# Narrow value products first behind transposes, sample sums in three pieces, and position products placed inside output products, in a two-layer encoder

## The chip, the cores and the metric

The kernel runs on 1 core of a Trainium2 chip. The metric is the device time of one execution in microseconds. The engines are named as in the profile: PE is TensorE (matmuls and transposes), PEld its weight loads, DVE is VectorE, ACT is ScalarE, POOL is GpSimd, SP is SyncE, which issues most DMAs.

## What is computed

Two sequences, 2048 prompt rows and 512 sample rows of 1024 float32 channels, go through two layers and a final norm:

```
h = rmsnorm(x, g);  z = h @ w_in            # layer 0: q, k, v, gate
o = banded_gqa_with_sink(q, k, v, ...)      # 16 heads, 4 kv heads, |i-j| <= 128
x = x + (o * silu(gate)) @ w_out
h = rmsnorm(x, g)                           # layer 1: 4 groups of 256 channels
f = fftn(h by group, axes=(positions, channels), norm="ortho").real
x = x + (f * silu(h @ w_gate)) @ w_out
y = rmsnorm(x, final_norm)
```

## The kernel before

Every float32 operand of a large product is split into a high part (a cast to the matmul's format on ACT) and a low part (the difference, on DVE), and each product is made of three matmuls: high by high, high by low, low by high (`matmul3`, L131 to L136; its rows are at L134).

**Attention.** Five chunks of 512 positions; the first is the sample. A chunk has 19 steps, and inside a step a table fixes the order of the pieces on every engine: first half of the values (AV1), transposes of the probabilities S of the next pair of blocks (T0, L709), second half of the values (AV2), scores (L650), the softmax pieces, and projection products that fill in between. The transposed probabilities are split into `pts`. The value products (`values`, L728 to L773, matmul at L767) work on the two halves of the 128 rows at the same time. Their weights are the values v, and for each block of keys two forms occur: part 0 loads 128 weight columns (high and low part of v) and multiplies with the high part of `pts`; part 1 loads 64 weight columns (the high part of v) and multiplies with the low part. They add up in `av`, the wide ones in 128 rows, the narrow ones in the first 64. The order of a half is the list at L745: the middle block wide, the far, the edge, then the three narrow ones. In the second half (`swap`) each half of the rows works for the other of the two blocks.

**Fourier.** Positions are transformed by radix-4 sums of 16 (prompt) or 4 (sample) residue classes, each an array of 128 x 1024. Pairs of classes are handled in turn: `gates(pr, hooks)` makes the products of one pair with the work of others hung in at numbered hooks, `z_odd_even` and L1402 make the channel transform, `combine` (L1599) joins two pairs by `radix4` (group 0: the sample) or `radix4_relative` and stores the sums by POOL DMAs in DRAM. Later, for each class k1, `position` (L1694) makes the position transform: `halves_of` splits the input into `gp` (cast at L1685 on ACT, difference at L1686 on DVE), products `ABp` (L134) go to PSUM, ACT copies (L1719), DVE combines (L1723 to L1726) and multiplies by the stored gate (L1729): the result is `up`. `step` (L1957) makes the positions of its arguments, then `finish` (L1762) for the class before, whose output products are `fo` (48 matmuls at L134 for 128 rows, with weights `tTu`; the weight pieces `wo0` to `wo15` are the moving operand), with the residual added at L1776 and the final norm at L1746. Then `up` is transposed on PE (L112) and split again (L1270 ACT, L1271 DVE). `emit` calls `step` for 0 and 8, then 4, then 2. The sums e, f, r0 and the differences G[4] for these classes are DVE operations at L1519.

In this phase the instructions are put in order by a scheduler, except where `seq` or `after(instruction, other)` fixes it; each engine runs its own in that order.

Of the kernel before, what the change touches and what calls it, by code (L numbers as in the profile page):

```python
# [55 lines left out]
def encoder(  # L56
# [147 lines left out]
    def attention_phase():  # L204

        with ExitStack() as es:
# [403 lines left out]
            def attention(c, p, res, uTs):  # L610
# [117 lines left out]
                def values(b):  # L728
# [12 lines left out]
                    def reached(i, h):  # L741
# [3 lines left out]
                        order = [(1, 0), (far, 0), (edge, 0), (1, 1), (edge, 1), (far, 1)]  # L745
                        rows = ahead = slice(64 * h, 64 * h + 64)
# [12 lines left out]
                    def half(swap):  # L759
                        todo = [reached(h ^ swap, h) for h in range(2)]  # L760
# [472 lines left out]
    def fourier_phase(tail):  # L1233
        with ExitStack() as es:
# [14 lines left out]
            def zt(name):  # L1249
                return right([P, D], F32, name)  # L1250
# [267 lines left out]
            def tt(out, a, b, op):  # L1518
                DVE.tensor_tensor(out, a, b, op)  # L1519
# [11 lines left out]

            def radix4(z, name):

                e = zt(f"e{name}")
                tt(e, z[0], z[2], ALU.add)
                tt(z[0], z[0], z[2], ALU.subtract)
                tt(z[2], z[1], z[3], ALU.add)
                tt(z[1], z[1], z[3], ALU.subtract)
                tt(z[3], e, z[2], ALU.subtract)
                tt(e, e, z[2], ALU.add)  # L1540
                return e, z[3], z[0], z[1]

# [56 lines left out]
            def combine(pr):  # L1599

                if pr.n % 2 == 0:
                    return
                gi = pr.n // 2
                r = (radix4_relative if pr.n > 1 else radix4)(pairs[pr.n - 1].zs + pr.zs, f"r{gi}")
# [3 lines left out]
                for i in range(4):  # L1608
                    POOL.dma_start(gsd[i] if gi == 0 else evd[gi - 1, i] if i < 2 else odd[gi - 1, i - 2], r[i])

            kept = []

# [22 lines left out]
            for n, pr in enumerate(pairs[:-1]):  # L1635
                nx = pairs[n + 1]

                def ahead_of(n, i):
# [5 lines left out]

                gates(pr, {
                    1: [lambda: turns1(nx)], 2: [lambda: turns2(nx)], 3: [lambda: turns3(nx)], 4: [lambda: turns4(nx)],
# [47 lines left out]
            def position(name, tab, gr, gs, tiles, loads=None, parts=None, between=None, later=None):  # L1694
# [4 lines left out]
                for hf in range(2):  # L1699
# [4 lines left out]
                    def acc(out, tabs, c0, n):  # L1704
                        for i, (w, t) in enumerate(zip(tabs, ts)):
# [4 lines left out]
                            end = matmul3(out, w, v, i == 0, i == len(ts) - 1)  # L1710
# [51 lines left out]
            def finish(uT, r, between=None):  # L1762
                r0 = r[0]
                x2 = residual(r)
                for half in range(2):
# [4 lines left out]
                    for k in range(KD):  # L1770
# [3 lines left out]
                        )  # L1774
                    xs = x2[:, half * 512 : half * 512 + 512]
# [287 lines left out]
            def emit(*ks):  # L2063
                step(*((f"p{k1}", k1, *G[k1], pair(k1, 16, 0)) for k1 in ks))
# [228 lines left out]
```

## Time and profile before

| what | value |
|---|---|
| runs | 1543.08, 1545.18, 1551.4 us |
| median | 1545.18 us |
| the profiled execution | 1545.72 us, its span 1543.2 us |
| mean granted clock of PE | 0.998 |
| instructions on PE, DVE, ACT, POOL | 13150, 2431, 1921, 616 |

A row of a timeline gives a start, a duration and a group of like instructions by engine, line, operation, `out<-in` and count; in brackets stands how long the engine was idle before it and what released it. The duration of a matmul reaches from its issue to the end of its write, so neighbouring ones overlap, and the pace is read from start to start. A row of groups gives total busy time, mean ns of one, and idle time before it. A row of windows gives the length and the busy time of PE, PEld, DVE, ACT and POOL, then the granted clock (1.00 is full speed), the DMA share and GB/s.

### The profile page before, as it was taken

What the parts mean: (1) busy time and instruction counts of PE and PEld (TensorE: products, weight loads), DVE (VectorE), ACT (ScalarE), POOL (GpSimd) and SP (SyncE); (2) the same over time, 40 slices, a digit from 0 to 9 for tenths busy, and PEclk for the clock granted to TensorE, in tenths of its full rate; (3) what the DMA queues carried; (4) which work ended last, traced back from release to release, by engine and by line L of the source; (5) the groups of instructions that cost most, each with busy time, mean ns of one, the idle gap of its engine ahead of it and who ended that gap; (6) DMA issues with size and microseconds to landing.
All of it is one profiled execution on the core that took longest, in us unless ns stands there. A gap on an engine that the chain in (4) does not pass through costs nothing.

```text
span 1543.2 us, 33658 instructions
## 1 busy us (share of the span) xinstructions
PE 1525.3 (99%) x13150; PEld 1331.4 (86%) x13150; DVE 1124.2 (73%) x2431; ACT 888.4 (58%) x1921; POOL 451.5 (29%) x616
## 2 busy tenths in 40 slices
PE   9999999999999999999999999999999999999998
PEld 7999888999898888988888899888888888788886
DVE  5898665777538776468764477667888878889896
ACT  6788534787237884268862477646656654343353
POOL 2566652422413323215124142222112111011100
PEclk9999999999999999999999999999999999999999
DMA  8677687685856766866649666684667679457852
GB/s 325 229 288 249 230 338 271 219 302 171 317 205 228 243 220 235 300 202 225 228 160 381 226 210 231 215 299 160 240 207 244 212 250 411 154 189 272 297 184 93
DMA packets 100729, 372.70 MB, mean 242 GB/s; under 512 B 11235, under 2 KB 22251, under 8 KB 83420
## 3 DMA queue, kind: packets, MB, share of 16 engines
q1 hardware_dynamic: 82716, 297.38, 55.8%
q0 software_dynamic: 16688, 70.04, 11.6%
q10 hardware_dynamic: 1168, 3.15, 0.6%
q8 instruction: 103, 1.69, 0.4%
q14 instruction: 54, 0.44, 0.1%
HBM read 280.06 MB, written 90.47 MB: 240 GB/s over the span
## 4 chain that ended last, share of the span: by engine, by line
PE 86%; DVE 6%; DMA 4%; ACT 2%; issue 1%; POOL 0%; SPq 0%; POOLq 0%; DVEq 0%; ACTq 0%
PE pj L524 27%; PE W L134 6%; PE pj L134 6%; PE av L767 6%; PE tp L134 5%; PE av L134 5%; PE spt L650 5%; PE spt L134 4%; PE tp L709 3%; PE Wo L134 3%; PE Z L134 3%; PE fo L134 3%; PE z L1402 2%; PE Zo L134 2%; PE X L134 1%; PE ABp L134 1%
## 5 line engine op out<-in xcount | busy, mean ns | idle before, releaser
L524 PE MATMUL pj<-h,wg 64*128 64x512 f32 x1920 | 438.6, 389 | 0.0
L524 PE MATMUL pj<-h,wq 64*128 64x512 f32 x1560 | 378.9, 389 | 1.2 <-DVE qab L568 1.2
L524 PEld LDWEIGHTS pj<-h,wg 64*128 64x128 f32 x1920 | 330.6, 184 | 20.4
L524 PEld LDWEIGHTS pj<-h,wq 64*128 64x128 f32 x1560 | 284.4, 184 | 22.8 <-DVE qab L568 2.7
L677 ACT ACTIVATE S<-S 128x385 f32<-128x385 f32 (+1 forms) x320 | 189.1, 592 | 61.8 <-DVE S L669 42.0
L669 DVE CUSTOM_DVE_ANT_0 S<-spt,b 128x385 f32<-128x385 f32 (+1 forms) x320 | 165.0, 525 | 79.5 <-PE spt L650 78.3
L722 ACT CAST pts<-tp 128x768 fp32r<-128x768 f32 (+1 forms) x160 | 121.2, 758 | 79.5 <-PE av L767 46.2
L726 DVE TENSOR_TENSOR pts<-tp,pts 128x768 fp32r<-128x768 f32 (+1 forms) x160 | 144.1, 900 | 10.7 <-ACT pts L722 10.1
L767 PE MATMUL av<-pts,v 64*128 64x256 f32 (+3 forms) x1680 | 123.8, 267 | 2.4 <-DVE pts L726 2.3
L812 POOL TENSOR_TENSOR uT<-o,uT 128x256 fp32r<-128x256 f32 x75 | 56.9, 758 | 231.3 <-ACT uT L808 230.9
L650 PE MATMUL spt<-kwin,qab 64*128 64x384 f32 (+1 forms) x960 | 119.5, 339 | 0.9 <-DVE S L669 0.7
L134 PE MATMUL fo<-wo,tTu 128*128 128x512 f32 x480 | 115.4, 394 | 0.0
L767 PEld LDWEIGHTS av<-pts,v 64*64 64x64 f32 (+1 forms) x1680 | 108.4, 159 | 7.4 <-DVE pts L726 3.1
L134 PEld LDWEIGHTS fo<-wo,tTu 128*128 128x128 f32 x480 | 89.1, 189 | 18.0
L709 PEld LDWEIGHTS tp<-ident,S 64*128 64x128 f32 x1792 | 86.6, 138 | 10.7 <-DVE pts L726 3.1
L709 PE MATMUL tp<-ident,S 64*128 64x64 f32 x1792 | 91.1, 223 | 0.2 <-DVE pts L726 0.2
L692 DVE TENSOR_SCALAR S<-S 128x384 f32<-128x384 f32 (+1 forms) x192 | 89.1, 493 | 0.1
L803 POOL TENSOR_TENSOR o<-o,s 128x256 f32<-128x256 f32 x75 | 55.6, 741 | 114.7 <-DVE o L797 89.8
L650 PEld LDWEIGHTS spt<-kwin,qab 64*128 64x128 f32 x960 | 81.5, 186 | 3.8 <-issue 1.8
L279 DVE SCALAR_TENSOR_TENSOR h<-xk,g0s,h 128x512 fp32r<-128x512 f32 x40 | 44.9, 1135 | 49.6 <-ACT h L278 49.6
L524 PE MATMUL pj<-wo,uT 64*128 64x512 f32 x360 | 74.6, 390 | 0.0
L278 ACT ACTIVATE h<-xk,g0s 128x512 fp32r<-128x512 f32 x40 | 28.7, 724 | 75.0 <-POOL xk L274 73.8
(376 smaller groups left out, 3358.5 us busy)
## 6 DMA issues: line engine op xcount, KB each, us to landing
wo<-wsd SPq DMA_DIRECT2D x32, 1024.0 KB, 6.5
wq<-wsd SPq DMA_DIRECT2D x31, 1024.0 KB, 6.6
wg<-wsd SPq DMA_DIRECT2D x31, 1024.0 KB, 5.7
x<-x1d SPq DMA_DIRECT2D x40, 512.0 KB, 4.0
b<-b21d SPq DMA_DIRECT2D x40, 512.0 KB, 5.2
b<-rowd SPq DMA_DIRECT2D x40, 384.0 KB, 4.2
xs<-in_x_dram SPq DMA_DIRECT2D x23, 512.0 KB, 6.3
s2d<-gt POOLq DMA_DIRECT2D x40, 256.0 KB, 4.4
```

Source lines behind the costliest of these rows:

```text
L134: ins = pe(PE.matmul(out, a[i], b[j], start=start and i + j == 0, stop=stop and i == 1, skip_group_check=more))
L524: out.last[h] = pe(PE.matmul(out.ps, a[i], b[j], **out.flags()))
L650: pe(PE.matmul(spt[j][:, 2 + k0 * P : 2 + k1 * P], res["q"][rows, qp, b * P : (b + 1) * P], kwin[g][rows, kp, b * P + k0 * P : b * P + k1 ...
L669: seq(DVE, DVE.tensor_tensor_reduce(out=s[:, e0:e1], in0=ps[:, 1 + e0 : 1 + e1], in1=st["bias"][:, j, 386 - e1 : 386 - e0][:, ::-1], scale ...
L677: last_exp[0] = seq(ACT, ACT.activation(s[:, e0:e1], s[:, e0:e1], AF.Exp, bias=s[:, 386:387], scale=-1.0, accum_out=s[:, 387:388]))
L692: seq(DVE, DVE.tensor_scalar(s[:, ks], s[:, ks], den, None, ALU.mult))
L709: pe(PE.transpose(ps[h][:, kb, j, :], s[rows, j, 1 + kb * P : 1 + (kb + 1) * P], ident[rows, rows]))
L722: seq(ACT, ACT.copy(hi, ps))
L726: seq(DVE, DVE.tensor_tensor(lo, ps, f32(hi), ALU.subtract))
L767: last[i][h] = pe(PE.matmul(to, v, pt, start=not swap and n == 0, stop=swap and n == len(todo[h]) - 1, skip_group_check=True,))
L803: eng.tensor_tensor(o, o, s, ALU.mult)
L812: low = eng.tensor_tensor(lo, o, f32(hi), ALU.subtract)
```

## The change

It has three parts.

First, in the second half of the values (`swap`), the list begins with the middle block's narrow product. The list of the first half stays.

```
-                    def reached(i, h):
+                    def reached(i, h, swap):
...
                         order = [(1, 0), (far, 0), (edge, 0), (1, 1), (edge, 1), (far, 1)]
+                        if swap:
+                            order = [(1, 1), (1, 0), (far, 0), (edge, 0), (edge, 1), (far, 1)]
...
-                        todo = [reached(h ^ swap, h) for h in range(2)]
+                        todo = [reached(h ^ swap, h, swap) for h in range(2)]
```

PE's rows at one second half, before (chunk 2, head pair 3; 128x256 and 64x256 are partitions and columns of the output, hence weight columns and streamed columns; v2_5 and v1_4 are the middle blocks):

```order
L709 MATMUL tp_79<-ident_81,S2_3_2_7500 128x64 x12
L767 MATMUL av_80<-pts2_3_0_7441,v2_5_6365 128x256
L767 MATMUL av_80<-pts2_3_0_7441,v1_4_3466 128x256
L767 MATMUL av_80<-pts2_3_0_7441,v2_6_6368 128x256
L767 MATMUL av_80<-pts2_3_0_7441,v1_3_3439 128x256
L767 MATMUL av_80<-pts2_3_0_7441,v1_4_3466 128x2x64
L767 MATMUL av_80<-pts2_3_0_7441,v2_5_6365 128x2x64
L767 MATMUL av_80<-pts2_3_0_7441,v2_5_6365 64x256
L767 MATMUL av_80<-pts2_3_0_7441,v1_4_3466 64x256
```

And after (the line has become L769):

```order
L709 MATMUL tp_79<-ident_81,S2_3_2_7500 128x64 x12
L769 MATMUL av_80<-pts2_3_0_7441,v2_5_6365 64x256
L769 MATMUL av_80<-pts2_3_0_7441,v1_4_3466 64x256
L769 MATMUL av_80<-pts2_3_0_7441,v2_5_6365 128x256
L769 MATMUL av_80<-pts2_3_0_7441,v1_4_3466 128x256
L769 MATMUL av_80<-pts2_3_0_7441,v2_6_6368 128x256
L769 MATMUL av_80<-pts2_3_0_7441,v1_3_3439 128x256
L769 MATMUL av_80<-pts2_3_0_7441,v1_4_3466 128x2x64
L769 MATMUL av_80<-pts2_3_0_7441,v2_5_6365 128x2x64
```

The two narrow products of the middle block have moved from behind the six wide ones to directly behind the transposes. In the attention phase nothing else moves on PE, and nothing on DVE, ACT, POOL or SP.

Second, the sample's sums (six DVE operations and four POOL DMAs) leave `combine` at hook 6 of pair 0's gates and stand in three pieces at hooks 2, 3 and 4 of pair 1's.

```
-                if pr.n % 2 == 0:
+                if pr.n % 2 == 0 or pr.n == 1:
                     return
...
+            def sample_sums(part):
...
+                if part == 0:
+                    tt(e, z[0], z[2], ALU.add)
+                    tt(z[0], z[0], z[2], ALU.subtract)
+                elif part == 1:
+                    tt(z[2], z[1], z[3], ALU.add)
+                    tt(z[1], z[1], z[3], ALU.subtract)
+                else:
+                    tt(z[3], e, z[2], ALU.subtract)
+                    tt(e, e, z[2], ALU.add)
+                    for i, r in enumerate((e, z[3], z[0], z[1])):
+                        POOL.dma_start(gsd[i], r)
...
-                    1: [lambda: turns1(nx)], 2: [lambda: turns2(nx)], 3: [lambda: turns3(nx)], 4: [lambda: turns4(nx)],
+                    1: [lambda: turns1(nx)], 2: [lambda: turns2(nx), lambda: sample_part(0)],
+                    3: [lambda: turns3(nx), lambda: sample_part(1)], 4: [lambda: turns4(nx), lambda: sample_part(2)],
```

In the order that results, DVE's rows there are the same but for one cast (S1_2, L1355), which stands four places earlier, and POOL's stores of the sums stand where they stood.

Third, `step` gets a number n. It issues the loads of its positions and the first casts, and `finish` calls the positions after its n-th output product, with their products tied behind that one (`behind`). The two differences of G[4] follow `emit(10, 0, 8)`, tied behind a DVE combination of the position 8; position 6's first casts move ahead of two sums.

```
-            def finish(uT, r, between=None):
+            def finish(uT, r, between=None, within=None, n=0):
...
+                        if within and half * KD + k + 1 == n:
+                            chain["rows"] = end
+                            within()
+                            chain.pop("rows")
...
-                            end = matmul3(out, w, v, i == 0, i == len(ts) - 1)
+                            end = matmul3(out, w, v, i == 0, i == len(ts) - 1, behind=chain.get("rows"))
...
-            def step(*positions):
-                new = [t for p in positions for t in position(*p)]
-                if pend:
-                    end = finish(*pend.pop(0))
+            def step(n, *positions):
+                new, held = [], []
+                for i, p in enumerate(positions):
+                    held.append((position_loads(p[0], p[1], p[4]), None if i else [halves_of(p[0], p[2], p[3], 0), None]))
+
+                def within():
+                    for p, h in zip(positions, held):
+                        new.extend(position(*p, *h))
+
+                if not n:
+                    within()
+                end = finish(*pend.pop(0), None, within, n)
...
-            e, g4r = pm(w0[0], w0[2], "e0")
-            f, g4s = pm(w0[1], w0[3], "f0")
+            e, f = zt("e0"), zt("f0")
+            for n, a, b in ((e, 0, 2), (f, 1, 3)):
+                tt(n, w0[a], w0[b], A)
             r0, r8 = pm(e, f, "r0")
-            G[0], G[8], G[4] = (r0, None), (r8, None), (g4r, g4s)
-            emit(0, 8)
+            G[0], G[8], G[4] = (r0, None), (r8, None), (w0[0], w0[1])
+            emit(10, 0, 8)
+            for a in range(2):
+                after(tt(w0[a], w0[a], w0[a + 2], S), last_b[0])
...
-            emit(4)
+            emit(0, 4)
...
-            emit(2)
+            emit(3, 2)
...
+            p6 = [halves_of("p6", *G[6], 0), None]
             g1s = zt("g1s")
             tt(g1s, o0s, e0s, A)
             g7s = [half_of(o0s, e0s, lower_half, "g7s0")]
             tt(o0s[:, upper_half], o0s[:, upper_half], e0s[:, upper_half], S)
-            p6 = [halves_of("p6", *G[6], 0), None]
```

PE's rows from the start of the output products of rows 2048 on (`fo2048`), in which positions 0 and 8 fall, before:

```order
L134 MATMUL fo2048_0_17997<-wo0_17430,tTu2048_0_17751 128x512 x3
L134 MATMUL fo2048_0_17997<-wo1_17432,tTu2048_0_17751 128x512
L134 MATMUL ABp0_0_17939<-gp0_0_0_17936,tbp0_17933 128x260
L134 MATMUL fo2048_0_17997<-wo1_17432,tTu2048_0_17751 128x512 x2
L134 MATMUL ABp0_1_17952<-gp0_1_0_17949,tbp0_17933 128x260
L134 MATMUL fo2048_0_17997<-wo2_17454,tTu2048_0_17751 128x512 x3
```

And after, from the tenth weight piece on:

```order
L134 MATMUL fo2048_1_17968<-wo9_17691,tTu2048_0_17751 128x512 x3
L134 MATMUL ABp0_0_17976<-gp0_0_0_17933,tbp0_17931 128x260 x3
L134 MATMUL ABp0_0_17976<-gp0_0_0_17933,tbp0_17931 128x256 x3
L134 MATMUL ABp0_1_17989<-gp0_1_0_17986,tbp0_17931 128x260 x3
L134 MATMUL ABp0_1_17989<-gp0_1_0_17986,tbp0_17931 128x256 x3
L134 MATMUL fo2048_1_17968<-wo10_17722,tTu2048_0_17751 128x512 x3
L134 MATMUL fo2048_1_17968<-wo11_17725,tTu2048_0_17751 128x512
L134 MATMUL ABp8_0_18004<-gp8_0_0_18001,tbp8_17938 128x260 x3
```

The first product of position 0 stood behind 4 of the 48 output products and now stands behind 30; the 12 of position 0 stand together, then 4 output products, the 12 of position 8, and the last 14. In the step of position 4 its 24 products stood together ahead of the next 48 output products; now 5 stand first, and 12 and 10 output products stand between the parts that follow (11 and 8). For position 2, 5 stood ahead of 5 output products and 19 behind; now 9 output products go first and the 24 stand together.

DVE's rows ahead of position 0, before (ev0_0 and ev1_0 are w0[0] and w0[1], e0, f0 and r0 the sums):

```order
L1519 TENSOR_TENSOR e0_17922<-ev0_0_17910,ev2_0_17914 128x1024
L1776 TENSOR_TENSOR x2_2049_17763<-x2_2049_17763,fo2049_1_17791 128x512
L1519 TENSOR_TENSOR ev0_0_17910<-ev0_0_17910,ev2_0_17914 128x1024
L1271 TENSOR_TENSOR tTu2050_0_17842<-tw0_17825,tTu2050_0_17842 128x512
L127 TENSOR_SCALAR invf2049_17820<-ssf2049_17817 128x1
L1519 TENSOR_TENSOR f0_17925<-ev1_0_17912,z11_17370 128x1024
L1746 SCALAR_TENSOR_TENSOR x2_2049_17763<-x2_2049_17763,invf2049_17820,gfb_17400 128x1024
L1271 TENSOR_TENSOR tTu2050_1_17845<-tw0_17825,tTu2050_1_17845 128x512
L1776 TENSOR_TENSOR x2_2051_17848<-x2_2051_17848,fo2051_0_17850 128x512
L1519 TENSOR_TENSOR ev1_0_17912<-ev1_0_17912,z11_17370 128x1024
L1519 TENSOR_TENSOR r0_17928<-e0_17922,f0_17925 128x1024
```

And after, further down, around position 8's gating (up8 times s2p8):

```order
L1740 TENSOR_TENSOR up8_0_18000<-up8_0_18000,ABp8_0_18004 128x2x127
L1740 TENSOR_TENSOR up8_0_18000<-up8_0_18000,ABp8_1_18017 128x2x127
L1741 TENSOR_TENSOR up8_0_18000<-up8_0_18000,ABp8_0_18004 128x2x127
L1741 TENSOR_TENSOR up8_0_18000<-up8_0_18000,ABp8_1_18017 128x2x127
L1521 TENSOR_TENSOR ev0_0_17910<-ev0_0_17910,ev2_0_17914 128x1024
L1744 TENSOR_TENSOR up8_0_18000<-up8_0_18000,s2p8_8_17936 128x1024
```

The two differences in place (ev0_0, ev1_0) stood ahead of r0 and are gone there; the first now stands between position 8's combinations and its gating, the second four rows behind the first. On the other engines the loads of a step's gates and tables are issued earlier: on SP one store of output rows (x2_0) now stands ahead of the load s2p2_2.

More of the change, by code (lines that the diff above doesn't have):

```diff
@@ L1518, in tt @@
             def tt(out, a, b, op):
-                DVE.tensor_tensor(out, a, b, op)
+                return DVE.tensor_tensor(out, a, b, op)
             def radix4_relative(z, name):
@@ L1608, in combine @@
                 for i in range(4):
-                    POOL.dma_start(gsd[i] if gi == 0 else evd[gi - 1, i] if i < 2 else odd[gi - 1, i - 2], r[i])
+                    POOL.dma_start(evd[gi - 1, i] if i < 2 else odd[gi - 1, i - 2], r[i])
             kept = []
+            def sample_sums(part):
+                z = pairs[0].zs + pairs[1].zs
+                if not part:
+                    kept_e.append(zt("er0"))
+                e = kept_e[0]
+                if part == 0:
[9 more added lines that the diff above has]
+                        POOL.dma_start(gsd[i], r)
+            kept_e = []
             pr = pairs[0]
```

18 lines of the change are left out of this document (6 added, 12 removed).

## The prediction

> **What bounds the kernel now.** I read the page's busy times and its chain first, then PE's waits, then the lines by form, and last the timelines at the places that the diff touches.
>
> ```profile
> span 1543.2 us, 33658 instructions
> PE 1525.3 (99%) x13150; PEld 1331.4 (86%) x13150; DVE 1124.2 (73%) x2431; ACT 888.4 (58%) x1921; POOL 451.5 (29%) x616
> PE 86%; DVE 6%; DMA 4%; ACT 2%; issue 1%; POOL 0%; SPq 0%; POOLq 0%; DVEq 0%; ACTq 0%
> PE ABp L134 <- ACT gp L1685: 2.1, 1, 2.1
> PE ABp L134 <- DVE gp L1686: 1.2, 2, 0.8
> PE z L1402 <- DVE s L1348: 1.1, 1, 1.1
> ```
>
> PE is busy for 1525.3 of 1543.2 us and makes up 86% of the chain, so about 18 us (1543.2 − 1525.3) of idle time can go at the most. What a change removes in PE's own stream counts in full; work moved on VectorE (DVE) counts only where PE waits for it. The last three rows (total us, times, longest) are the waits near the edited code: position products for casts, and the columns of pair 2 for a sum. A busy PE can still hold time that weight loads cost, so the next rows are the value products, by tile and shape. The POOL row counts their sites: one such sum for each.
>
> ```profile
> L767 PEld LDWEIGHTS av<-pts,v 64*128 64x128 f32 x840 | 71.7, 186 | 4.3 <-ACT S L690 0.4 <-issue 0.2
> L767 PEld LDWEIGHTS av<-pts,v 64*64 64x64 f32 x840 | 54.8, 132 | 3.1 <-DVE pts L726 3.1
> L803 POOL TENSOR_TENSOR o<-o,s 128x256 f32<-128x256 f32 x75 | 55.6, 741 | 114.7 <-DVE o L797 89.8 <-PE pj L524 24.9
> ```
>
> **Part 1, value products.** One site in the timeline of PE (start, duration of the group, instructions): first half, 12 transposes, second half, scores.
>
> ```profile
> 493.93 0.75 PE L767 MATMUL av<-pts,v 64*128 64x256 f32 x12
> 494.52 0.53 PE L709 MATMUL tp<-ident,S 64*128 64x64 f32 x12
> 494.87 0.84 PE L767 MATMUL av<-pts,v 64*128 64x256 f32 x12
> 495.55 0.69 PE L650 MATMUL spt<-kwin,qab 64*128 64x384 f32 x6
> ```
>
> Both halves stream the same columns. From start to start the first half takes 494.52 − 493.93 = 0.59 us, the second 495.55 − 494.87 = 0.68. The first comes behind 512-column products, long enough to hide its first weight loads; the second comes behind transposes of 64 columns, which hide little. So about 0.09 us of loading lies bare at a site. A 64-column load takes 186 − 132 = 0.054 us less, and the change puts that load first: 75 x 0.054 = 4.05 us. Bounds: nothing (the next, longer load is bare instead) and the whole 0.09, 75 x 0.09 = 6.8 us.
>
> Against it: the second half now goes from 128-wide transposes to a 64-wide product, back to 128 and to 64 again, two more changes of width at a site. The first half contains one such change. The 12 products stream 4 x 256 + 2 x 128 columns at each width, 2560 in all, two at a time on the two halves of the rows: 1280. At the output products' pace of 0.23 us for 512 columns (rows below) that is 0.575 us, so the change of width fits into 0.59 − 0.575 = 0.015 us, about the rounding of the rows. Two at each site would be at most 2.3 us; I take off 0.25 us, near the small end, and keep 2.3 for the range. Part 1: −3.8 us.
>
> The Trainium skill ("TensorEngine Tiling (Array Packing)", section "Key Properties") says that going over to another tiling mode drains TensorE. It speaks against this edit; the first half's 0.59 us shows no drain of a size that matters, but its price is a rival below.
>
> **Part 2, sample sums.** They leave the end of pair 0's gates and come in three pieces during pair 1's. VectorE's queue comes out the same but for one cast (S1_2) four places earlier, and the stores of the sums stay in place on POOL's queue. So on the path they cost and gain nothing. The wait near them is this:
>
> ```profile
> 1087.41 0.47 PE L1402 MATMUL z<-chan_sb,S 128*128 128x256 f32 x2 [1.06 <-DVE s L1348]
> ```
>
> Its bounds are −1.06 (gone) and, were one VectorE operation of 1.22 us (rows below) put ahead of it, about +1.2.
>
> **Part 3, positions 0 and 8.** PE's timeline, then the granted clock (the 1.00 and the 0.51, third from the end) in two stretches:
>
> ```profile
> 1311.74 2.65 PE L134 MATMUL fo<-wo,tTu 128*128 128x512 f32 x11
> 1316.45 0.39 PE L134 MATMUL ABp<-gp,tbp 128*128 128x260 f32 x1 [2.05 <-ACT gp L1685]
> 1326.29 4.93 PE L134 MATMUL fo<-wo,tTu 128*128 128x512 f32 x21
> 1331.15 1.21 PE L112 MATMUL tw<-ident,up 64*128 64x64 f32 x32
> 1311.00:1314.00 3.00, 3.00 (x14) 2.47 (x14) 3.00 (x4) 0.00 (x0) 0.00 (x0) 1.00 0.63 257
> 1317.20:1320.60 3.40, 3.40 (x13) 2.94 (x12) 2.84 (x5) 1.80 (x4) 0.86 (x1) 0.51 0.40 136
> 1343.32 3.06 PE L134 MATMUL ABp<-gp,tbp 128*128 128x260 f32 x24
> 1346.21 11.07 PE L134 MATMUL fo<-wo,tTu 128*128 128x512 f32 x48
> ```
>
> Of the 11 output products in the first row 4 belong to this step; then PE waits 2.05 us for the cast of the sum r0, and behind the wait runs at half the clock for 3.4 us, which loses 1.7 us more. The change puts 26 further output products there, and the wait is covered if r0's cast is done by then. Working at full pace: an output product takes (1331.15 − 1326.29)/21 = 0.23 us, a position product (1346.21 − 1343.32)/24 = 0.12. The first row's 11 end at 1311.74 + 11 x 0.229 = 1314.25, and the next ones now go on: 26 x 0.229 = 5.95 to 1320.2; 12 ABp0, 1.44; 4 fo, 0.92; 12 ABp8, 1.44, to 1324.0; 14 fo, 3.2, to 1327.2. There the transposes stood at 1331.15: −3.95 us. The cover holds, since r0 comes earlier:
>
> ```profile
> 1307.52 1.22 DVE L1519 TENSOR_TENSOR ev<-ev,ev 128x1024 f32<-128x1024 f32 x1
> 1308.65 0.68 DVE L1271 TENSOR_TENSOR tTu<-tw,tTu 128x512 fp32r<-128x512 f32 x1
> 1314.53 1.22 DVE L1519 TENSOR_TENSOR r<-e,f 128x1024 f32<-128x1024 f32 x1
> 1315.78 1.14 ACT L1685 CAST gp<-r 128x512 fp32r<-128x512 f32 x2 [5.82 <-DVE r L1519]
> 1320.77 0.38 ACT L1719 COPY up<-ABp 128x258 f32<-128x258 f32 x1 [1.77 <-PE ABp L134]
> 1322.11 0.74 DVE L1726 TENSOR_TENSOR up<-up,ABp 128x254 f32<-128x254 f32 x2
> 1323.37 1.22 DVE L1729 TENSOR_TENSOR up<-up,s2p 128x1024 f32<-128x1024 f32 x1
> ```
>
> A subtraction holds VectorE for 1308.65 − 1307.52 = 1.13 us, and two leave the queue ahead of r0. Its casts, now done at 1315.78 + 1.14 = 1316.9, are due before 1315, some 5 us before PE asks; even at 1316.9 they would be covered.
>
> What is late next: one of the moved subtractions now stands ahead of position 8's gating. Its last product ends at about 1324.15; copy 0.38, three combinations left at 0.37 each, the subtraction 1.13, the gating 1.22, with some 0.1 of hand-over: 1328.05. Its transposes come due 16 of them after 1327.2, at (half of the 1.21 us) 1327.75: a new wait of 0.3, where none was. Part 3: −3.95 + 0.3 = −3.65 us. From both sides: no wait and −3.95; and two VectorE operations later, a wait of 2.6 and −1.4.
>
> The Trainium skill ("TensorE: Matmul & The Clock Gate", section "HAM oscillation — how this bites in real kernels") has PE fall to a slow clock only after more than 3.4 us of idling. The trace differs: 2.05 us were followed by 0.51. By the page the 1.7 us would not be this wait's, and the total would be −5.5 instead of −7.2.
>
> **Part 4, positions 4, 2 and 6.** At 1343.32 the 24 products of position 4 stand together. Now five come first, then 12 output products, and the rest in two parts. PE arrives about 3.7 us earlier, and the subtracted inputs, their second half's casts and combinations are one or two operations later on VectorE. The nearest rows are the waits of 0.39 and 0.79 us of the same kind:
>
> ```profile
> 1371.71 2.56 PE L134 MATMUL ABp<-gp,tbp 128*128 128x260 f32 x19 [0.39 <-DVE gp L1686]
> 1402.36 0.63 PE L134 MATMUL ABp<-gp,tbp 128*128 128x260 f32 x3 [0.79 <-DVE gp L1686]
> 1357.32 0.69 DVE L1776 TENSOR_TENSOR x<-x,fo 128x512 f32<-128x512 f32 x1 [4.05 <-PE fo L134]
> 1369.23 1.22 DVE L2098 SCALAR_TENSOR_TENSOR z<-z,tm 128x1024 f32<-128x1024 f32 x1
> 1370.97 0.69 DVE L1686 TENSOR_TENSOR gp<-g2s,gp 128x512 fp32r<-128x512 f32 x1
> ```
>
> For position 4 I take +0.5, between nothing (the 12 output products last 2.75 us) and the 3.65 that would give part 3 back. At 1357.32 VectorE idles 4.05 us for PE, so a PE that is 3.2 us early finds it with slack, and what lies behind moves along. There position 2's cast of g2s goes ahead of a 1.22 us operation, and position 6's casts go ahead of others: −0.2 of the 1.18 us, with ends −1.2 and +1.2. The loads issued earlier on SP's queue change place with one store and delay nothing that PE waits for here.
>
> **The sum.** −3.8 + 0 − 3.65 + 0.5 − 0.2 = −7.15, say −7.2 us. The profiled execution took 1545.72 us (1543.2 of it the span), 0.54 above the median of the runs, 1545.18. It would come to 1538.5, and the median to **1538.0 us**. About 0.5% (7.7 us, to 1537.45) is what a measurement here can tell from no change: the forecast lies just inside.
>
> **The rivals.**
>
> *Widths cost (the slower side).* Each change of tile width drains PE for the difference between a matmul's duration and its issue: 277 ns in the row below less 115 for 256 columns (half of 0.23) is 0.16 us. Two more at 75 sites: 150 x 0.16 = +24, less the 7.2: about 1562 us. It decides from 7.2/150 = 0.048 us a change. Against it stand the 0.59 us of the first half, 0.015 over the stream with such a change within. 4%.
>
> ```profile
> L767 PE MATMUL av<-pts,v 64*64 64x256 f32 x570 | 75.9, 277 | 2.4 <-DVE pts L726 2.3
> ```
>
> *VectorE takes part 3 back.* It is the next bound: the moved subtractions are not removed, and positions 4, 2 and 8 wait for it instead. Part 3 falls from −3.65 to −0.65: about 1541 us. For it stands the window below (its third busy time, 106.16 of 120 us, is VectorE's); against it the 4.05 us idle at 1357.32. 17%.
>
> ```profile
> 1300.00:1420.00 120.00, 116.77 (x666) 96.77 (x665) 106.16 (x152) 40.01 (x77) 14.81 (x18) 0.99 0.59 211
> ```
>
> *The load stays hidden or bare anyway.* If the wait that ends last in the second half is for the values, or the second load is bare in place of the first, part 1 is nothing: −3.4, 1541.8 us. 8%.
>
> *All of it pays and more.* The bare 0.09 goes whole at part of the sites, or the waits at 1087.41, 1371.71 and 1402.36 go too (−1.06 − 1.0): −9, about 1536 us. 16%.
>
> That the sums are spread without effect is in the forecast itself, since the queue hardly changes.
>
> **How the numbers follow.** Forecast 1538.0, 55%, its own range 1536.5 to 1539.5 (the 2.3 of the widths on one side, waits on the other); it straddles 1537.45, and I give 26 of the 55 to faster. All of the 16% of the last rival is faster: 42%. Within 0.5% are 29 + 17 + 8 = 54%; slower 4%. The range 1534.5 to 1542.5 leaves out the slower rival and the tails of both neighbours, together under 2 in 10.
>
> **What would show it.** Right: the second half at its sites takes 0.62 to 0.64 us from start to start instead of 0.68, the idle 2.05 us and the 0.51 are gone, the transposes come about 4 us earlier against the step's first product, and the 1.06 stays. Wrong: the second half is at 0.68 or above (part 1), a wait above 1 us at position 8's transposes or position 4's products (part 3), or matmuls of over 0.28 us where the width changes.

## The result, and the profile after

The changed kernel takes 1541.51 us in the median of 20 runs (1539.54 to 1544.59), the kernel before 1545.07 (20 runs beside them, 1542.59 to 1551.40). The ratio is 0.9973, with a 95% interval of 0.9964 to 0.9981: about 4.2 us faster, by the medians 3.6. That lies in the range 1534.5 to 1542.5, but above the forecast's own 1536.5 to 1539.5, and it is little more than half of the 7.2 us forecast. The profiled execution took 1541.41 us, its span 1539.2, 4.0 less than before.

The head of the page, its chain and PE's waits over 0.5 us (total, times, longest), after:

```profile
span 1539.2 us, 33657 instructions
PE 1522.1 (99%) x13150; PEld 1329.9 (86%) x13150; DVE 1122.6 (73%) x2431; ACT 888.1 (58%) x1921; POOL 453.9 (29%) x616
PE 87%; DVE 7%; issue 2%; ACT 2%; DMA 1%; POOL 0%; POOLq 0%; ACTq 0%; DVEq 0%; SPq 0%
PE av L769 <- DVE pts L726: 2.3, 2, 1.2
PE z L1404 <- DVE s L1350: 1.2, 1, 1.2
PE ABp L134 <- DVE gp L1701: 0.7, 2, 0.3
PE ABp L134 <- DVE invf L127: 0.6, 1, 0.6
```

The 2.1 us for the cast on ACT is gone, and the 1.1 at the columns of pair 2 is there still (1.2). The site of the second half, in PE's timeline after:

```profile
493.30 0.75 PE L769 MATMUL av<-pts,v 64*128 64x256 f32 x12
493.89 0.53 PE L709 MATMUL tp<-ident,S 64*128 64x64 f32 x12
494.23 0.79 PE L769 MATMUL av<-pts,v 64*64 64x256 f32 x12
494.86 0.69 PE L650 MATMUL spt<-kwin,qab 64*128 64x384 f32 x6
```

The first half takes 493.89 − 493.30 = 0.59 us as before, the second 494.86 − 494.23 = 0.63 instead of 0.68. The value products as a whole, of the kernel before and then of the changed one (after the durations stand the starts of the first and the last):

```profile
L767 PE MATMUL av<-pts,v x1680: 215/275/387, 52.2 to 993.6; 64*64 64x256 f32 x60, 64*128 64x256 f32 x56, 64*64 64x128 f32 x37, 64*128 64x128 f32 x34
```

```profile
L769 PE MATMUL av<-pts,v x1680: 215/275/395, 51.7 to 991.1; 64*128 64x256 f32 x65, 64*64 64x256 f32 x58, 64*64 64x128 f32 x38, 64*128 64x128 f32 x26
```

They last 993.6 − 52.2 = 941.4 us before and 991.1 − 51.7 = 939.4 after: 2.0 less, where 75 times 0.05 would be 3.75. The missing 1.75 us is about what one stretch of half clock costs (3.41 us at half the pace, 1.7), and there is one in the first chunk. Two stretches of the window view of the changed kernel (length, busy time of PE, PEld, DVE, ACT and POOL, granted clock, DMA share, GB/s):

```profile
86.51:89.92 3.41, 2.24 (x32) 1.57 (x31) 3.34 (x11) 3.29 (x9) 3.10 (x5) 1.00 0.66 224
89.92:93.33 3.41, 3.41 (x25) 3.41 (x24) 3.25 (x11) 2.68 (x7) 1.77 (x3) 0.50 0.96 251
```

In the first PE waits 1.15 us for `pts`, as it does in the kernel before at the same instruction (1.16); in the second it runs at half the clock. In the profiled execution before, it did so not here but behind the 2.05 us wait. Then positions 0 to 6 (PE's timeline after):

```profile
1304.64 13.54 PE L134 MATMUL fo<-wo,tTu 128*128 128x512 f32 x59
1318.02 1.61 PE L134 MATMUL ABp<-gp,tbp 128*128 128x260 f32 x12
1319.47 1.10 PE L134 MATMUL fo<-wo,tTu 128*128 128x512 f32 x4
1320.41 1.71 PE L134 MATMUL ABp<-gp,tbp 128*128 128x260 f32 x12
1321.96 3.36 PE L134 MATMUL fo<-wo,tTu 128*128 128x512 f32 x14
1325.25 1.52 PE L112 MATMUL tw<-ident,up 64*128 64x64 f32 x32
1326.70 11.18 PE L134 MATMUL fo<-wo,tTu 128*128 128x512 f32 x48
...
1352.12 1.20 PE L112 MATMUL tw<-ident,up 64*128 64x64 f32 x32
...
1368.60 1.90 PE L134 MATMUL ABp<-gp,tbp 128*128 128x260 f32 x11 [0.57 <-DVE invf L127]
...
1394.52 0.63 PE L134 MATMUL ABp<-gp,tbp 128*128 128x260 f32 x3 [0.34 <-DVE gp L1701]
...
1400.98 0.64 PE L134 MATMUL ABp<-gp,tbp 128*128 128x260 f32 x3 [0.31 <-DVE gp L1701]
...
1426.16 3.02 PE L134 MATMUL Wo<-fT,S 128*128 128x512 f32 x12 [0.32 <-DVE x L1869]
```

No wait and no slow clock at position 0; the transposes stand at 1325.25 (1331.15 before) and last 1326.70 − 1325.25 = 1.45 us instead of 1.14, since position 8's gating is 0.3 late. The ledger of the 4.0 us, by rows that stand above and in the prediction: from the start to the last value product −2.5 (993.6 to 991.1, 0.5 of it ahead of the first one); from there to the transposes of position 0 −3.4 (337.55 us before, 334.15 after); from these to the end of the span **+1.9** (1543.2 − 1331.15 = 212.05 before, 1539.2 − 1325.25 = 213.95 after). So 1.9 us, nearly the size of the 2.05 us wait, is given back behind it.

### The profile page after: what moved, and what is told of

It is laid out like the page before. It is cut to its first block, busy times and chain, and to the rows that moved or that the text cites. A ratio compares the mean times of both kernels' runs of the same rounds, so it can differ in the third digit from the quotient of the medians.

```text
span 1539.2 us, 33657 instructions
## 1 busy us (share of the span) xinstructions
PE 1522.1 (99%) x13150; PEld 1329.9 (86%) x13150; DVE 1122.6 (73%) x2431; ACT 888.1 (58%) x1921; POOL 453.9 (29%) x616
## 4 chain that ended last, share of the span: by engine, by line
PE 87%; DVE 7%; issue 2%; ACT 2%; DMA 1%; POOL 0%; POOLq 0%; ACTq 0%; DVEq 0%; SPq 0%
PE pj L524 27%; PE W L134 6%; PE pj L134 6%; PE tp L134 5%; PE av L769 5%; PE av L134 5%; PE spt L650 5%; PE spt L134 4%; PE tp L709 3%; PE Wo L134 3%; PE Z L134 3%; PE fo L134 2%; PE z L1404 2%; PE Zo L134 2%; PE X L134 2%
## 5 line engine op out<-in xcount | busy, mean ns | idle before, releaser
L769 PE MATMUL av<-pts,v 64*128 64x256 f32 (+3 forms) x1680 | 120.3, 262 | 2.4 <-DVE pts L726 2.3
L769 PEld LDWEIGHTS av<-pts,v 64*128 64x128 f32 (+1 forms) x1680 | 104.9, 159 | 7.2 <-DVE pts L726 3.1
```

Source lines behind the costliest of these rows:

```text
L769: last[i][h] = pe(PE.matmul(to, v, pt, start=not swap and n == 0, stop=swap and n == len(todo[h]) - 1, skip_group_check=True,))
```

## The experiments

Each was timed in five rounds beside the kernel before. Since half clock turned out to come in some executions and not in others, the runs are also sorted by the mean granted clock of each. One stretch of 3.41 us at half clock lowers it by 3.41 x 0.5/1543 = 0.0011, and the half clock at the end of every span, where PE has run dry, lowers it by a changing amount. In the 14 profiled executions the mean is 0.9985 to 0.9995 without such a stretch and 0.9975 to 0.9982 with one. So 0.999 is an execution with none, 0.998 mostly one but now and then none (the order alone's profiled execution is such a case), and 0.997 or less at least one.

```
kernel                     runs  0.999  0.998  less   mean span of the runs at 0.999
before (four batches)        95     35     24    36   1541.7
changed                      20     10     10     0   1538.4
order alone                   6      2      3     1   1538.3
positions alone              12      8      4     0   1541.7
sums alone                   12      4      4     4   1541.8
widths alternate             12      7      2     3   1544.8
low parts early               6      5      1     0   1538.4
differences on POOL          12      5      5     2   1539.4
positions at five            12      6      4     2   1538.4
low parts late               12      0      9     3   -
no last scale                 6      6      0     0   1534.9
early low, seven              8      5      3     0   1537.3
order, early low             12      6      4     2   1539.0
early low, six               12      9      2     1   1537.6
```

The 95 runs of the kernel before have mean spans of 1541.7 at 0.999, 1543.4 at 0.998, 1544.4 at 0.997 and 1546.3 at 0.996: each step of 0.001 costs about 1.5 us.

**Order alone.** Only the list of the second half is changed.

```
+                        if swap:
+                            order = [(1, 1), (1, 0), (far, 0), (edge, 0), (edge, 1), (far, 1)]
```

> The kernel before with the first part of the change alone (narrow product first in the second half). Theory (shorter load): each of the 75 sites is 0.05 us shorter, so the attention phase ends about 3.9 us earlier, 1541.2 us in the median; a half-clock window of 3.4 us behind the 1.15 us wait at about 88 us comes in about half of the executions of every kernel, this one or not, and is worth 1.5 us. Rival (the order lowers PE's activity): the half-clock window at 90 us comes with the narrow product, in nearly every execution of this kernel, and the gain is 2.4 us: 1542.7. Rival (no gain, the load is bare anyway): 1545.

Measured: 1540.52 us against 1545.34, ratio 0.9961 (0.9947 to 0.9975); without half clock its span is 1538.3 against 1541.7, −3.4. Only two of the six runs are at 0.999; the changed kernel against the positions alone, which differ by the order and the sums, says the same with ten and eight runs (1538.4 against 1541.7, −3.3). The load theory holds. That the order itself brings the half clock (first rival) is not borne out: 4 of 6 executions here lie below 0.999, of the kernel before 60 of 95, and six runs are too few for more. In its profiled execution, at 0.998, the 2.05 us wait was 1.4 and no half clock followed it or any other wait; it also held a wait of 2.4 us, of transposes for a division, that the other profiles do not have.

**Positions alone.** Only `step`, `emit`, and the moved casts and subtractions.

> The kernel before with the third part alone (positions inside the output products). Theory: the 2.05 us wait and the half clock behind it go, 3.5 us, and 1.0 to 1.5 of it is given back at positions 4, 2 and 6 and at the last transform, where VectorE and a load are late: the net gain is 2.0 to 2.5 us, 1542.6 to 1543.1 in the median. Rival (the give-back came from the attention phase being earlier, through the DMAs): the full 3.5 stays, 1541.6.

Measured: 1543.95 us, ratio 0.9990 (0.9980 to 1.0000). At 0.999 its span is that of the kernel before, 1541.7: the wait is saved and wholly given back. What it gains is the clock: 4 of 12 executions lie below 0.999 instead of 60 of 95. The gain is smaller than either expectation, and the give-back is there without the earlier attention phase, so the rival falls.

**Sums alone.** Only the sample's sums.

> The kernel before with the second part alone (sample sums in three pieces). Theory: VectorE's queue changes by one cast, so nothing: 1545 within 0.5 us; the 1.06 us wait in the product of pair 2 stays within 0.3. Rival (the cast that goes ahead makes that wait longer and the pair's products late): slower by 0.3 to 0.5 us.

Measured: 1545.36 us, ratio 1.0001 (0.9989 to 1.0012), as forecast. It gave more: its profiled execution had the wait at position 0 (2.3 us) and no half clock. The stretch of the clock's grid that holds most of the wait, and the next:

```profile
1314.86:1318.28 3.42, 1.91 (x9) 1.63 (x10) 3.42 (x6) 2.58 (x5) 0.05 (x1) 1.00 0.49 149
1318.28:1321.69 3.41, 3.41 (x20) 2.76 (x20) 2.96 (x7) 1.41 (x4) 1.40 (x2) 1.00 0.13 26
```

The grid cut the wait in two, and PE was busy for 1.91 us of the first stretch. In the kernel before it lay in one stretch:

```profile
1313.73:1317.14 3.41, 1.36 (x6) 0.80 (x6) 3.41 (x4) 1.36 (x3) 0.00 (x0) 1.00 0.34 108
1317.14:1320.55 3.41, 3.41 (x12) 2.95 (x12) 2.90 (x5) 1.86 (x4) 0.86 (x1) 0.50 0.40 136
```

**Widths alternate.** The second half goes narrow, wide, narrow, wide, narrow, wide.

```
-                            order = [(1, 1), (1, 0), (far, 0), (edge, 0), (edge, 1), (far, 1)]
+                            order = [(1, 1), (1, 0), (edge, 1), (far, 0), (far, 1), (edge, 0)]
```

> As the order alone, but the second half goes narrow, wide, narrow, wide, narrow, wide: six changes of width at a site instead of four (two in the kernel before). Theory (a change of width costs at most 0.015 us): the same gain as the order alone, less at most 2.3 us: 1541.2 to 1543.5. Rival (a change of width drains PE, 0.16 us): 150 more of them are 24 us, 1565.

Measured: 1547.41 us, ratio 1.0018 (1.0006 to 1.0029); at 0.999 1544.8, 6.5 us above the order alone, more than the theory's 2.3 and far from the rival's 24. One site:

```profile
290.80 0.86 PE L769 MATMUL av<-pts,v 64*64 64x256 f32 x12
291.50 0.74 PE L650 MATMUL spt<-kwin,qab 64*128 64x384 f32 x6
```

It takes 291.50 − 290.80 = 0.70 us; the same site takes 0.65 in the changed kernel (290.45 to 291.10). Start by start, the products on one half of the rows follow each other here at 0.12 and 0.06 us (their streams of 256 and 128 columns) through every change of width but two, where 0.17 stands: at the head, as in the changed kernel, and at a wide load behind the narrow product of 128 columns, whose 0.06 us are too short to hide it. That is 75 x 0.05 = 3.8 of the 6.5 us. The scores too now start behind a product of 128 columns, and their six take 0.57 us to the next matmul (291.50 to 292.07) instead of 0.52 (291.10 to 291.62): as much again, if it holds at every site. Together that is more than the 6.5; the difference was not followed up. So a change of width by itself costs nothing that shows, and a load longer than the stream ahead of it does, as at the head of the half.

**Low parts early.** In the first chunk's table VectorE makes the low parts of `pts` ahead of two bias operations.

```
-... ("B", 0), ("b2a", 0), ("m1b", 0), ("W", 0), ("b2b", 0), ("lo1", 1), ("e2a", 0), ...
+... ("B", 0), ("lo1", 1), ("b2a", 0), ("m1b", 0), ("W", 0), ("b2b", 0), ("e2a", 0), ...
```

> The changed kernel, and in the first chunk's table the low parts of the second transposes (the DVE operation on which PE waits twice for 1.15 us, at about 70 and 88 us) stand ahead of the bias operations of the other block. Theory (a half-clock stretch follows a 3.41 us stretch of the clock's own grid in which PE streamed less than about a third of its columns, and only the two waits of the first chunk still make such stretches in the changed kernel): the waits shrink to 0.3 us or less, hardly any execution has a half-clock stretch (mean clock 0.999 in nearly all instead of in half), and the median goes down by 1.5 to 1.8 us for the waits and some 0.8 for the clock: 1539.0. Rival (the stretches come from elsewhere, or at random): the waits go, 1.5 to 1.8 us, but 0.998 stays in half of the executions. Other rival (the bias operations are then late and PE waits for the exponentials): no gain, 1541.5.

Measured: 1540.53 us (6 runs), ratio 0.9967 (0.9954 to 0.9981). PE's waits:

```profile
PE tp L709 <- DVE S L696: 1.7, 2, 0.9
PE av L769 <- DVE pts L726: 0.4, 2, 0.2
```

The wait for `pts` shrinks from 2.3 to 0.4 us, and the transposes wait 1.7 us for the division instead: VectorE is full there (3.34 of 3.41 us in the changed kernel's stretch above), so no wait is saved (1538.4 at 0.999, as the changed kernel). What changed is where it falls; 5 of 6 executions had no half clock. With the two candidates below, which have the same edit, it is 19 of 26, so the stretches have become rarer but not gone.

**Low parts late.** The same operation behind a division instead.

```
-... ("b2b", 0), ("lo1", 1), ("e2a", 0), ("m1a", 0), ...
+... ("b2b", 0), ("e2a", 0), ("m1a", 0), ("lo1", 1), ...
```

> The changed kernel with the low parts of the second transposes of the first chunk one place later on VectorE, behind a division: the two waits at about 70 and 88 us grow from 1.15 to some 1.6 us. Theory (a half-clock stretch follows when PE streamed less than a third of its columns within one of the clock's 3.41 us): most executions now have one or two stretches, mean clock 0.998 or 0.997 in at least three of four (0.999 in half of them for the changed kernel), and the median is 1.0 us slower for the waits and 1 to 1.5 us for the clock: 1543.5 to 1544. Rival (the stretches fall at random): 0.999 stays in half of the executions, 1542.5.

Measured: 1543.21 us, ratio 0.9993 (0.9982 to 1.0004), and of 12 executions not one at 0.999 (10 of 20 for the changed kernel). The profiled one shows it in the stretch with the 1.55 us wait and the next:

```profile
87.52:90.93 3.41, 1.86 (x33) 1.60 (x32) 3.38 (x12) 2.65 (x9) 3.21 (x5) 1.00 0.63 176
90.93:94.34 3.41, 3.41 (x21) 3.41 (x19) 3.15 (x11) 2.67 (x7) 1.33 (x2) 0.50 0.90 297
```

So the stretches come from the waits, not at random. That the place of the clock's grid decides which executions have them fits the two traces shown under the sums alone; it was not followed from run to run.

**Differences on POOL.** The two moved subtractions are POOL's. Their tie behind position 8 goes with the edit, so they stand early, ahead of position 0.

```
-                after(tt(w0[a], w0[a], w0[a + 2], S), last_b[0])
+                POOL.tensor_tensor(w0[a], w0[a], w0[a + 2], S)
```

> The changed kernel with the two moved subtractions for position 4 on POOL instead of VectorE. Theory (VectorE's work between the positions 0 and the last transform is what gives the 2.05 us back, at 0.3, 0.5, 0.5 and 0.4 us): 2.26 us of VectorE's work less, and the four waits shrink together by 1 us or more: 1540.4. Rival (each wait has a cause of its own, a product's place or a load): no change, 1541.5; or slower by up to 1 us where POOL's 3 us operations stand ahead of the small norms for which VectorE waits.

Measured: 1543.33 us, ratio 0.9988 (0.9977 to 0.9999), 1.8 above the changed kernel. It says nothing for or against VectorE as the bound, since it did not relieve it. VectorE's and then POOL's timeline:

```profile
1304.39 3.05 DVE L1521 TENSOR_TENSOR f<-ev,z 128x1024 f32<-128x1024 f32 x1
1309.70 3.41 DVE L1761 SCALAR_TENSOR_TENSOR x<-x,invf,gfb 128x1024 f32<-128x1024 f32 x1 [0.47 <-POOL invf L128]
```

```profile
1303.96 2.40 POOL L2100 TENSOR_TENSOR ev<-ev,ev 128x1024 f32<-128x1024 f32 x1 [6.05 <-DVE e L1521]
1309.65 2.38 POOL L2100 TENSOR_TENSOR ev<-ev,z 128x1024 f32<-128x1024 f32 x1
```

The operations of VectorE that ran beside POOL's took 3.05 and 3.41 us instead of 1.22 and 1.28: 1.8 and 2.1 more, together more than the 2 x 1.13 that the subtractions take on VectorE. A wait of 2.94 us at position 8 came besides, whose releaser the profile does not name; its cause stays open. The expectation's gain did not come.

**Positions at five.** Positions 0 and 8 stand behind the 5th output product.

```
-            emit(10, 0, 8)
+            emit(5, 0, 8)
```

> The changed kernel with positions 0 and 8 behind the 5th instead of the 10th output product. Their casts are done at 1315.0, PE would ask at about 1314.6, and VectorE idles 1.5 us at 1317.8 for them. Theory (VectorE gives the 2.05 us back): the idle time is used, position 8's gating is done long ahead of its transposes, and the waits behind shrink by 1 us or more: 1540.3. Rival (the number hardly matters): 1541.5; a wait of up to 0.5 us for the casts at position 0 may come.

Measured: 1541.95 us, ratio 0.9981 (0.9972 to 0.9991), and 1538.4 at 0.999, as the changed kernel: in the mean the rival is right. The profiled execution is the shortest of these (1536.5) and went in part as the theory says:

```profile
1323.95 1.21 PE L112 MATMUL tw<-ident,up 64*128 64x64 f32 x32
1325.09 11.19 PE L134 MATMUL fo<-wo,tTu 128*128 128x512 f32 x48
1336.12 3.46 PE L134 MATMUL ABp<-gp,tbp 128*128 128x260 f32 x24
```

The 0.3 at position 8's transposes is gone and position 4's products stand together, though one of them follows its neighbour at 0.36 us instead of 0.12. Position 8's products come 0.3 us late instead (1315.63, with four output products from 1314.40 ahead of them). And 6 of the 12 executions lie below 0.999, and the spans at 0.999 go from 1536.5 to 1539.9. With five products ahead of them, position 0's products have little left to cover late inputs; that this is what spreads the runs was not measured.

**No last scale.** The last multiplication of the final norm on VectorE is left out, so the output rows are not scaled.

```
-                    ins = placed("dve", DVE.scalar_tensor_tensor(x2, x2, inv[:, 0:1], gfb, ALU.mult, ALU.mult))
-                    after(ins, last_b[0])
```

> The changed kernel without the last multiplication of the final norm (one VectorE operation of 1.28 us for each block of output rows; the output is left unscaled). Theory (VectorE's work between the positions 0 and the last transform gives back what the 2.05 us wait gained): eight such operations fall there, about 9 us of VectorE's 107, so the waits of 0.3, 0.5, 0.6 and 0.4 us go or shrink to a third, and the time goes down by 1 to 1.5 us: 1540.2. Rival (product order and loads set these waits): no change, 1541.5, with waits of 1.5 us or more left between 1316 and 1430 us.

Measured: 1536.28 us (6 runs), ratio 0.9947 (0.9932 to 0.9962), 5.2 below the changed kernel. PE between position 0's transposes and position 2, and the window of both kernels, the changed one first:

```profile
1324.23 1.53 PE L112 MATMUL tw<-ident,up 64*128 64x64 f32 x32
...
1364.93 3.06 PE L134 MATMUL ABp<-gp,tbp 128*128 128x260 f32 x24
1367.82 9.03 PE L134 MATMUL fo<-wo,tTu 128*128 128x512 f32 x39
```

```profile
1316.00:1420.00 104.00, 102.55 (x594) 84.53 (x593) 94.05 (x135) 35.61 (x69) 14.29 (x13) 1.00 0.57 201
```

```profile
1316.00:1420.00 104.00, 103.90 (x606) 86.93 (x605) 88.50 (x134) 38.87 (x75) 14.85 (x13) 1.00 0.62 222
```

With VectorE at 88.50 us instead of 94.05, PE is busy for 103.90 of 104 us; the waits at positions 2 and 6 and at the last transform are gone, and from the transposes to the end it is 1534.8 − 1324.23 = 210.6 us instead of 213.95. The sizes go beyond the expectation (3.4 instead of 1 to 1.5), the cause is the one expected: VectorE's work behind position 0 gives the wait back. It is cleanest at position 2, whose 24 products stand behind the same 57 output products in both kernels and lose their wait of 0.57 us. At positions 4 and 6 the scheduler also placed the products otherwise among the output products (13 instead of 2 of position 6 stand first, for one), so there the work and the order are not told apart. The 0.3 at position 8's transposes, which was expected to go, stays (1325.69 − 1324.23 = 1.46 us). Some more of the 5.2 is clock: no stretch in 6 runs, which was not foreseen. The edit does not touch the first chunk, so that may be chance.

**Early low, seven; order, early low; early low, six.** Candidates: the changed kernel with the low parts early and positions 0 and 8 behind the 7th or 6th output product, and, for comparison, the order and the early low parts with the positions as before.

```
-            emit(10, 0, 8)
+            emit(7, 0, 8)
```

> A candidate: the changed kernel with the low parts of the second transposes earlier in the first chunk (few half-clock stretches) and positions 0 and 8 behind the 7th output product (between the 5th and the 10th, so that VectorE starts 1.9 us earlier and the casts are still covered). Theory: the clock is 0.999 in nearly all executions, and about 1 us of the later waits goes: 1539.5. Rival (the place of positions 0 and 8 makes no difference in the mean): 1540.5, as with the early low parts alone.

> The candidate (early low parts, positions 0 and 8 behind the 7th output product, 1539.1) with the 6th instead of the 7th. Theory (VectorE is the bound behind the positions 0, PE's place for them matters only through it): the same or 0.3 us less, 1539.0, below the changed kernel by 2 us or more. Rival (at the 6th PE already waits for the casts of position 0): 1540 or more, with a wait for casts at about 1315 us.

> The kernel before with the narrow product first and the low parts of the second transposes earlier in the first chunk, the positions as before. Theory (the positions' part is worth only the half-clock stretches behind the 2.05 us wait, since VectorE gives the wait itself back): in executions without a stretch (mean clock 0.999) the time is that of the changed kernel with early low parts, span 1538.4; a stretch behind the 2.05 us wait comes in a third to a half of the executions, so the median is 0.5 to 1 us above that kernel's 1540.5: 1541.2. Rival (the positions' part is worth its 2 us of wait in every execution): 1542.5, span 1540.4 at 0.999.

Measured: 1539.13 us (8 runs, ratio 0.9967, 0.9952 to 0.9981) with seven, 1539.83 (12 runs, 0.9964, 0.9952 to 0.9976) with six, 1541.75 (0.9975, 0.9964 to 0.9987) with the old positions. At 0.999 the spans are 1537.3, 1537.6 and 1539.0, the changed kernel's 1538.4. So the two candidates are below the changed kernel by 2.4 and 1.7 us in the median and by about 1 without half clock, but the intervals of the ratios overlap with its own. The clock of 0.999 in nearly all executions, expected with seven, did not come (5 of 8; with six 9 of 12), and with six neither expectation was met: 1539.83 instead of 1539.0, without a wait for the casts of position 0, but with one of 0.59 us at position 8 whose releaser the profile does not name. The third says what the positions' part is worth when the first chunk is quiet: 1539.0 − 1538.4 = 0.6 us (6 and 5 runs) and the clock, not the 2 us of the rival.

## Why the prediction was right and where it failed

**Part 1 held.** −3.8 us was forecast, −3.4 measured without half clock, and the site shows it: 0.63 for 0.68. The slower rival, a drain at each change of width, is refuted by the alternating order: its 150 further changes cost 6.5 us and not 24, and the part of it that was found lies at loads that a short stream leaves bare. By the drain rule of the Trainium skill ("TensorEngine Tiling (Array Packing)", section "Key Properties") the change should have lost; none of these traces shows a drain.

**Part 2 held**: nothing, and the wait stayed.

**Part 3 failed in one term.** "behind the wait runs at half the clock for 3.4 us, which loses 1.7 us more": this was taken as a sure part of the wait. It is there in some executions only: in the profiled one it was, in those of the order alone and the sums alone it was not, behind waits of 1.4 and 2.3 us. Over the runs, the kernel before has a mean clock of 0.9978 and the changed one of 0.9985; the difference, 0.0007/0.0011, is 0.6 of a stretch, 1.0 us; by the mean spans (4.05 less over all runs, 3.35 at 0.999) it is 0.7. The rest of the part came as worked out: no wait at position 0, 0.3 us at position 8's transposes, and from the step's first output product to the transposes 14.03 us instead of 17.82, 3.8 less where 3.95 was forecast.

**Part 4 failed in size.** "−0.2 of the 1.18 us" for positions 2 and 6, and nothing behind them. Position 4's +0.5 came (transposes at 1352.12 follow 26.87 us behind position 0's in the changed kernel, 26.06 before, 0.3 of the difference being the longer transposes). Positions 2 and 6 lost about half a microsecond in place of gaining 0.2, and the last transform another 0.4 (its row of x landed 4.1 us earlier, PE came 4.5 earlier). In all 1.9 us are given back where the sum had 0.6. The argument that VectorE has slack because it idles 4.05 us at 1357.32 was the wrong one: that slack is one place. Behind it, in the changed kernel from 1355.06 to 1406.75 us, just past position 6's products, VectorE is busy almost as long as PE (third and first busy time):

```profile
1355.06:1406.75 51.69, 50.44 (x267) 41.52 (x266) 50.10 (x68) 18.80 (x35) 7.38 (x5) 1.00 0.44 148
```

So the rival "VectorE takes part 3 back" came true: without half clock the positions' part gives nothing, 1541.7 for 1541.7 (0.6 us when the first chunk is quiet), and no last scale points to VectorE as the reason, most clearly at position 2. That the time also met the rival's price (about 1541 us) is partly luck, since the rival too counted the half clock as sure.

**The sum.** Measured −4.2 us: −3.4 for the loads, 0 for the sums, 0 net for the wait at position 0, and about −0.8 for rarer half clock. The forecast had −3.8, then −2.25 for the wait with +0.6 given back, and −1.7 for the clock. The profiled span's 4.0 agrees with this only by luck, since half clock fell on one place in either execution.

## What to carry to other kernels

A wait removed from the bound engine is worth only what the next engine lets it keep: add up that engine's work from there on, and do not take its idle time at one row for slack. One profiled execution shows one draw of the clock: sort the timed runs by mean clock before putting a slow stretch into a sum. And behind short streams put the shortest weight load first.

## What the runs showed of the hardware

Half clock came in stretches of 3.41 us on a grid of its own that lay elsewhere in each execution (the changes of the clock lie whole multiples of 3.413 us apart, 85.33 = 25 x 3.413 in the changed kernel), and always right behind a stretch in which PE streamed little. From the shapes of the matmuls in the traces, columns streamed in each stretch were counted, a product on 64 of the 128 rows as half: the three stretches followed by half clock in the middle of a kernel had 2308 (kernel before), 2560 (changed) and 2560 (low parts late); in the 14 profiled executions no stretch with 2624 or more was followed by it, though some held idle times of 1.5 us. At full pace (512 columns in 0.229 us) a stretch streams 7630, so in these traces the border lies at about a third. Counted without the weight of rows it does not separate them (5120 for the changed kernel's, 4104 for one without half clock). The Trainium skill ("TensorE: Matmul & The Clock Gate", section "Part 1: The HAM clock gate (the "warmup" mystery)") has a free-running window of 3413 ns, which these stretches agree with, and has PE go to half clock after an idle window; here a stretch with 2.24 us of busy PE was followed by half clock (changed kernel) and one with 1.91 was not (sums alone), so no wholly idle window was needed, and it is the columns streamed, not the busy time, that tells the cases apart. Three stretches followed by half clock are few; low parts late agrees with the rule over 12 executions, but no run tried the border itself.

Beside a 2.4 us operation of POOL with two inputs of 128 x 1024, VectorE's operation took 3.05 or 3.41 us instead of 1.22 or 1.28. The Trainium skill ("SBUF — State Buffer", section "SBUF: two separate sides") says that the two share a port pair under a lock. The trace agrees: both of VectorE's operations end 1.08 us behind the end of POOL's (1304.39 + 3.05 = 1307.44 behind 1303.96 + 2.40 = 1306.36, and 1309.70 + 3.41 = 1313.11 behind 1309.65 + 2.38 = 1312.03), about the 1.13 us that one of them takes alone, so they seem to have waited for the whole of it.
